# Asking for stored gate rows by pairs, and raising the priority of two steps, in a gated hybrid decoder step

## The chip, the cores and the metric

The kernel runs on one core of one Trainium2 chip. A core has a matrix engine (TensorE, PE here), a vector engine (VectorE, DVE), an engine for activations (ScalarE, ACT), GpSimd (POOL), and SyncE (SP), which here asks for nearly all DMA transfers. Each engine takes its own instructions in the order of the program and waits on semaphores for the others. The metric is the device time of one execution in microseconds (us); lower is better.

## The reference

One layer of a decoder step, on 1024 prompt tokens and on 64 sample tokens (8 requests of 8), with a model width of 1024. The sample tokens carry states; both groups use the same weights.

```
mod = silu(c) @ w_ada + b_ada                       # shifts, scales, gates
h = rmsnorm(x, g_norm1) * (1 + sc1) + sh1
rx, ry, sx, ga, gb = split(h @ w_in + b_in)
ra = rglru_branch(rx, ry, ...);  sb = s5_branch(sx, ...)
branch_a = ra @ w_rg_proj
glu_a, glu_b = split(sb @ w_glu)
branch_b = glu_a * sigmoid(glu_b)
merged = sigmoid(ga) * branch_a + sigmoid(gb) * branch_b
x = x + gt1 * (merged @ w_out)
h = rmsnorm(x, g_norm2) * (1 + sc2) + sh2
ua, ub = split(causal_dwconv(h @ w_up))
x = x + gt2 * ((gelu(ua) * ub) @ w_down);  y = rmsnorm(x, g_final)
```

The kernel computes the sigmoids as (tanh(v / 2) + 1) / 2. The change lies where `merged` is made and where the operands of `h @ w_up` are prepared.

## The kernel before

Everything is held transposed: eight row blocks m = 0 to 7 of 128 channels by tokens. The tokens go in two halves; half 0 is 512 prompt tokens and the 64 sample tokens (tiles of 128x576, two matmuls of 288 columns, L224), half 1 the other 512 prompt tokens (128x512, L226). Every fp32 operand is split into a hi and a lo part, and each product is three matmuls: hi by hi, lo by hi, hi by lo. For weights ACT makes the hi part (L176, `whi`) and DVE the lo part (L177, `wlo`) right after each load. For activations it is an ACT copy and a DVE subtraction too.

`strip` does two output blocks: it goes through the rows of X two at a time, and each chunk of weights serves two rows and two output blocks, 12 matmuls in half 1. After each chunk it calls `tick`, which lets background generators emit a few instructions. So background work and the main loop mix on the engines. The final order on each engine is set by a scheduler with priorities: an instruction has its place in program order, and `tc.high_priority(offset=k)` treats it as if it had been written k places earlier. Operands and buffers still bind.

The stretch that the change touches first is the GLU loop, one round for each pair b = 0 to 3 of row blocks. It multiplies by w_glu for columns 4 + b (gate side), and ACT puts the tanh into `q` (L1076). It multiplies for columns b (value side), and DVE makes (q + 1) * acc (L1081). Then for each of the two rows m it loads the stored gate row (`tgb`, written to DRAM earlier), makes (tgb + 1) * q (L1085), then 0.5 * q + bA (L1086), and splits the result into `mg` hi (ACT, L1088) and `mg` lo (DVE, L1089). `bA` is the other branch, made earlier. After the loop w_out multiplies `mg` (mg0 to mg7, in this order, two to a chunk) and adds the residual `xr`.

Loads into this loop and into the background generators share one tag of two buffers: `load_x` and `load_n` (L1095 to L1105) both take tag "ld". A third load thus waits until the first one's reader is done. In half 0's GLU a generator loads the second half's x (`xB`, later `xB2`) through these buffers, squares it (ACT, L347) and adds the squares into `accB` (DVE, L348), which PE sums over partitions (L357, `prs`). In half 1's GLU another generator (`h2a`) loads x after the first residual (`x2A`) through them and makes the operands `B11` and `B21` of the up-projection (L1157 ACT, L1158 DVE).

The up-projection multiplies 2 by 2 blocks in the manner of Strassen, with sums of activations as operands: `B11`, `B21`, `B22`, `T1` to `T4`, four row blocks each, made in `h2b` by a DVE subtraction (T3 at L1229, T4 at L1233) and the split (L1157, L1158). `up_lead` runs the first blocks while these are made, for two quads of output blocks; its last products are those with T2 (`p6`), with T3 (`p7`, L1251) and, for the first quad, with T4 (`p4`, L1248). DVE evacuates the results as `up` (L1405, L1408); a quad's `p4` writes where its `p7` has been evacuated. T4's forms live where the `h2B` tiles were, so T4 of a row can be made only after T3 of that row, and its second operand is loaded from DRAM (`hA`).

Of the kernel before, what the change touches and what calls it, by code (L numbers as in the profile page):

```python
# [8 lines left out]
F32 = mybir.dt.float32  # L9
F32R = mybir.dt.float32r  # L10
I32 = mybir.dt.int32
AF = mybir.ActivationFunctionType
OP = mybir.AluOpType
# [38 lines left out]
def _body(ctx, nc, tc, a):  # L52
    V, S, G, T_ = nc.vector, nc.scalar, nc.gpsimd, nc.tensor
# [157 lines left out]
    def strip(half, w, cb, X, nkb, kb0=0, tok=slice(0, 512)):  # L211

        T = [mm("mm0"), mm("mm1")] if half == 0 else [mm("mm")]
        for i, (hi, lo) in enumerate(weights(w, cb, range(kb0 // 2, (kb0 + nkb) // 2))):
            for m in range(2):
                c = slice(m * 128, (m + 1) * 128)
                for k in range(2):
                    x = X[2 * i + k]
                    first, last = i + k == 0, 2 * i + k == nkb - 1
                    for n, (y, r) in enumerate(((hi, 0), (hi, 1), (lo, 0))):  # L220
                        f = dict(start=first and n == 0, stop=last and n == 2)
                        if half == 0:
                            for h in range(2):
                                T_.matmul(T[m][:, h, :288], y[:, k, c], x[:, r, h * 288:(h + 1) * 288], **f)  # L224
                        else:
                            T_.matmul(T[0][:, m, tok], y[:, k, c], x[:, r, tok], **f)  # L226
            tick()
        return [Acc(half, T[m if half == 0 else 0], m) for m in range(2)]
# [799 lines left out]
    def part1(half, L, X, during_glu, ahead=None):  # L1028

        smp = half == 0  # L1030
        n = WID[half]
        sb = [None] * 4
        sxP = sx_strip(half, X, ahead)
        if smp:
            precompute_small()
        ra = [None] * 8
        H = []

        s5g = s5_blocks(half, sxP, sb)
        if not smp:  # L1040
            cold.append(s5g)
            other.append(adaB)
        for s in range(2):
            gate_strip(half, 0, s, X)
        for s in range(2):
            if s == 1 and smp:
                cold.append(s5g)
            g = rx_strip(half, s, X, H)
            gate_strip(half, 1, s, X)
            ry_strip(half, s, X, g, H, ra, L["RA"])  # L1050
        bA = []
        for b in range(4):
            if smp and b == 2:
                gt1 = ada_gen((4, 5), lambda: psum("ms", [128, 512], "sada"), adahl)
                other.append(gt1)
            acc = strip(half, a["w_rgp"], b, ra, 8)
            P2 = slot(L["BA"][b], f"bA{b}", F32)
            for j in range(2):
                m = 2 * b + j
                t = P2[:, j]  # L1060
                x = load_x(tgd[half][0][m * 128:(m + 1) * 128], "tga")
                with tc.high_priority(offset=400):
                    V.scalar_tensor_tensor(W(half, t), W(half, x), 1.0, acc[j].w, op0=OP.add, op1=OP.mult)
                bA.append(t)
        drain(s5g)
        if not smp:
            lead_weights()
        during_glu()
        merged = [None] * 8
        for b in range(4):  # L1070
            acc = strip(half, a["w_glu"], 4 + b, sb, 4)
            q = []
            for j in range(2):
                t = tmp("rx", [128, 664], f"q{j}", bufs=4)
                with tc.high_priority(offset=400):
                    S.activation(W(half, t), acc[j].w, AF.Tanh, scale=0.5)  # L1076
                q.append(t)
            acc = strip(half, a["w_glu"], b, sb, 4)
            for j in range(2):
                with tc.high_priority(offset=400):  # L1080
                    V.scalar_tensor_tensor(W(half, q[j]), W(half, q[j]), 1.0, acc[j].w, op0=OP.add, op1=OP.mult)  # L1081
            for j in range(2):
                m = 2 * b + j
                x, t = load_x(tgd[half][1][m * 128:(m + 1) * 128], "tgb"), q[j][:, :n]
                V.scalar_tensor_tensor(t, x, 1.0, t, op0=OP.add, op1=OP.mult)  # L1085
                V.scalar_tensor_tensor(t, t, 0.5, bA[m][:, :n], op0=OP.mult, op1=OP.add)  # L1086
                merged[m] = slot(L["MG"][m], f"mg{m}")
                S.activation(merged[m][:, 0, :n], t, AF.Copy, scale=0.5)  # L1088
                V.scalar_tensor_tensor(merged[m][:, 1, :n], t, 0.5, merged[m][:, 0, :n].bitcast(F32),  # L1089
                                       op0=OP.mult, op1=OP.subtract)  # L1090
        if smp:
            drain(gt1)
        return merged
# [6 lines left out]
    def load_x(src, name):  # L1100
        n = src.shape[1]
        t = (one("ld2", [128, 576], name, bufs=4) if two else tmp("ld", [128, 576], name, bufs=2))[:, :n]
        nc.sync.dma_start(t, src)
        return t
# [42 lines left out]
    def form(n, j):  # L1147
        if n in FORMS:
            x = slot(FORMS[n][j], f"{n}_{j}")
            x = x[:, :, :512] if n == "B22" else x  # L1150
        else:
            x = one(f"{n}_{j}", [128, 2, 512], f"{n}_{j}", F32R)
        F[n, j] = x
        return x

    def split_form(x, f):
        S.activation(x[:, 0], f, AF.Copy)  # L1157
        V.tensor_sub(x[:, 1], f, x[:, 0].bitcast(F32))  # L1158
# [48 lines left out]
    def h2b(ST):  # L1207

        A = []

        def load(tag, k, bufs):
            t = tmp(tag, [128, 632], "hA", bufs=bufs)[:, :576]
            nc.sync.dma_start(t, h2d[k])
            return t

        for j in range(4):
            norm_raw(ST[j][:, 1], ST[j][:, 1], rB2, 2 * j + 1)
            split_form(form("B22", j), ST[j][:, 1])
        for j in range(4):
            A.append(load("gl", 2 * j, 4))  # L1220
        for j in range(4):
            norm_raw(ST[j][:, 0], ST[j][:, 0], rB2, 2 * j)
            V.tensor_sub(A[j][:, 32:544], ST[j][:, 0], A[j][:, 32:544])
            split_form(form("T1", j), A[j][:, 32:544])
        for j in range(4):
            V.tensor_sub(A[j][:, 32:544], ST[j][:, 1], A[j][:, 32:544])
            split_form(form("T2", j), A[j])
        for j in range(4):
            V.tensor_sub(ST[j][:, 0], ST[j][:, 1], ST[j][:, 0])  # L1229
            split_form(form("T3", j), ST[j][:, 0])  # L1230
        for j in range(4):
            c = load("xc", 2 * j + 1, 3)
            V.tensor_sub(A[j], c, A[j])  # L1233
            split_form(form("T4", j), A[j])

    def prod(acc, kind, wt, n, start=False, stop=False):
        hi, lo = [x.rearrange("p (j c) -> p j c", c=128) for x in wt]
# [581 lines left out]
```

## Time and profile before

| | |
|---|---|
| median of 3 runs | 1747.87 us (1746.34 to 1749.92) |
| the profiled execution | 1748.04 us, its span in the trace 1746.3 us |
| PE busy | 1698.4 us, 97% |
| DVE busy | 1238.5 us, 71% |
| ACT busy | 913.3 us, 52% |
| DMA | 250.87 MB, 144 GB/s on average |

An engine's busy time is the sum of its instructions' durations. PE at 97% means that nearly all of the span is matmuls in a row, and that the other engines matter only where PE waits for them. A wait shows twice: in the list of waits, summed by the line that waited and what released it, and in the timeline, in brackets behind the instruction that came after it. Times in the timeline are counted from the start of the span. Line numbers in rows of the trace are those of the kernel before.

### The profile page before, as it was taken

Reading aid. Unit: us, or ns where it says so; the run is one execution under the profiler, and the core shown is the slowest. Engines: PE = TensorE matmul, PEld = TensorE weight load, DVE = VectorE, ACT = ScalarE, POOL = GpSimd, SP = SyncE. Lnnn points to the kernel's source line nnn. Section 1 sums busy time; section 2 is a strip of 40 time slices with the busy share of each in tenths; the row PEclk is TensorE's granted clock in tenths of the full one; section 3 lists DMA queues with packets and bytes.
Section 4 is the critical chain, followed back from the end, with each engine's and each line's share of the span. In section 5 each row is a group of like instructions: output and inputs, shape, how many; then the busy total and the mean of one; then the engine's idle time right before and its main releaser. Section 6 shows DMA issues by size and latency. Waiting matters only on the chain.

```text
span 1746.3 us, 29385 instructions
## 1 busy us (share of the span) xinstructions
PE 1698.4 (97%) x10542; PEld 1528.9 (88%) x10542; DVE 1238.5 (71%) x2629; ACT 913.3 (52%) x1608; POOL 230.6 (13%) x488
## 2 busy tenths in 40 slices
PE   7999999999999999999998999999999989999997
PEld 3899999998998777878786999999999979999887
DVE  8888688967855798665859877777777775336426
ACT  3556758535535588654536554555555545224224
POOL 0012110100100010020011422223322230000000
PEclk9999999999999999999999999999999999999999
DMA  8275334366546664455662222222222248445634
GB/s 305 70 237 178 97 109 145 105 196 209 178 145 195 210 190 147 122 157 162 217 224 94 77 81 81 80 75 75 75 75 74 76 136 287 133 134 172 195 95 136
DMA packets 151826, 250.87 MB, mean 144 GB/s; under 512 B 34048, under 2 KB 43264, under 8 KB 151680
## 3 DMA queue, kind: packets, MB, share of 16 engines
q1 hardware_dynamic: 151680, 248.99, 46.1%
q8 instruction: 83, 1.36, 0.3%
q14 instruction: 63, 0.52, 0.1%
HBM read 205.20 MB, written 43.73 MB: 143 GB/s over the span
## 4 chain that ended last, share of the span: by engine, by line
PE 69%; DVE 6%; DMA 3%; ACT 2%; issue 1%; POOLq 0%; SPq 0%; POOL 0%; DVEq 0%; ACTq 0%
PE mm L226 14%; PE mm L224 14%; PE b L1248 13%; PE e L1244 7%; PE mm L1541 7%; PE a L1248 4%; PE b L1251 3%; DMA al<-act 1%; DVE wlo L177 1%; PE pv L787 1%; PE pg L961 1%; DMA tgb<-tg 1%; PE sada L274 1%; PE sada L273 1%; DMA x2A<-x2d 1%
## 5 line engine op out<-in xcount | busy, mean ns | idle before, releaser
L176 ACT ACTIVATE whi<-raw 128x512 fp32r<-128x512 f32 x240 | 150.4, 627 | 218.8 <-PE mm L226 99.7
L177 DVE TENSOR_TENSOR wlo<-raw,whi 128x512 fp32r<-128x512 f32 x240 | 165.2, 689 | 123.6 <-ACT whi L176 103.7
L224 PE MATMUL mm<-h1A,whi 128*128 128x288 f32 x1024 | 182.9, 298 | 0.0
L226 PE MATMUL mm<-h1B,whi 128*128 128x512 f32 x512 | 159.8, 393 | 0.0
L177 DVE TENSOR_TENSOR wl<-raw,wh 128x512 fp32r<-128x512 f32 x105 | 72.0, 688 | 121.5 <-ACT wh L176 116.5
L224 PEld LDWEIGHTS mm<-h1A,whi 128*128 128x128 f32 x1024 | 151.1, 189 | 0.2
L224 PE MATMUL mm<-act,wh 128*128 128x288 f32 x768 | 135.8, 298 | 9.0 <-ACT act L1157 5.7
L176 ACT ACTIVATE wh<-raw 128x512 fp32r<-128x512 f32 x105 | 65.7, 628 | 143.1 <-PE mm L1541 81.7
L1248 PE MATMUL b<-T,wh 128*128 128x288 f32 x768 | 134.8, 296 | 4.8 <-DVE up L1408 1.8
L1541 PE MATMUL mm<-act,wh 128*128 128x512 f32 (+1 forms) x456 | 124.4, 361 | 0.0
L224 PEld LDWEIGHTS mm<-act,wh 128*128 128x128 f32 x768 | 114.2, 190 | 10.4 <-ACT act L1157 6.2
L1248 PEld LDWEIGHTS b<-T,wh 128*128 128x128 f32 x768 | 114.6, 188 | 8.4 <-DVE T L1158 2.1
L226 PEld LDWEIGHTS mm<-h1B,whi 128*128 128x128 f32 x512 | 95.6, 188 | 23.0
L245 ACT ACTIVATE wh<-wA 128x512 fp32r<-128x512 f32 x94 | 59.3, 630 | 105.5 <-PE b L1248 42.4
L224 PE MATMUL mm<-h1A,wlo 128*128 128x288 f32 x512 | 110.5, 296 | 2.5 <-DVE wlo L177 2.5
L246 DVE TENSOR_TENSOR wl<-wA,wh 128x512 fp32r<-128x512 f32 x94 | 65.3, 695 | 56.6 <-ACT wh L245 56.1
L226 PE MATMUL mm<-h1B,wlo 128*128 128x512 f32 x256 | 100.6, 393 | 0.7 <-DVE wlo L177 0.7
L1541 PEld LDWEIGHTS mm<-act,wh 128*128 128x128 f32 x456 | 80.7, 188 | 14.5 <-issue 0.5
L1386 DVE SCALAR_TENSOR_TENSOR gl<-up,vec,gl 128x624 f32<-128x624 f32 (+1 forms) x96 | 76.3, 806 | 14.2 <-ACT gl L1384 12.6
L1386 DVE SCALAR_TENSOR_TENSOR uc<-up,vec,uc 128x624 f32<-128x624 f32 (+1 forms) x96 | 75.8, 804 | 14.5 <-ACT uc L1384 11.4
L224 PEld LDWEIGHTS mm<-h1A,wlo 128*128 128x128 f32 x512 | 82.3, 188 | 2.7 <-DVE wlo L177 2.7
L224 PE MATMUL mm<-act,wl 128*128 128x288 f32 x384 | 83.2, 298 | 0.1
(452 smaller groups left out, 4351.1 us busy)
## 6 DMA issues: line engine op xcount, KB each, us to landing
raw<-w_in SPq DMA_DIRECT2D x128, 256.0 KB, 2.8
raw<-w_down SPq DMA_DIRECT2D x105, 256.0 KB, 2.7
wA<-w_up SPq DMA_DIRECT2D x94, 256.0 KB, 2.7
raw<-w_ada SPq DMA_DIRECT2D x56, 256.0 KB, 3.1
act<-uc SPq DMA_DIRECT2D x48, 256.0 KB, 2.1
araw<-w_ada SPq DMA_DIRECT2D x20, 512.0 KB, 7.2
s5a<-s5d SPq DMA_DIRECT2D x16, 512.0 KB, 4.0
raw<-w_rgp SPq DMA_DIRECT2D x32, 256.0 KB, 2.8
```

The lines of the kernel that those rows point to most:

```text
L176: S.activation(hi, raw, AF.Copy)
L177: V.tensor_sub(lo, raw, hi.bitcast(F32))
L224: T_.matmul(T[m][:, h, :288], y[:, k, c], x[:, r, h * 288:(h + 1) * 288], **f)
L226: T_.matmul(T[0][:, m, tok], y[:, k, c], x[:, r, tok], **f)
L245: S.activation(hi, src, AF.Copy)
L246: V.tensor_sub(lo, src, hi.bitcast(F32))
L273: T_.matmul(sa[:18], csr[:, kb], hi, start=kb == 0, stop=False)
L1244: T_.matmul(acc, w, x, **f)
L1248: T_.matmul(acc[:, h, :288], w, x[:, h * 288:(h + 1) * 288], **f)
L1251: T_.matmul(acc[:, h, o:o + 256], w, x[:, h * 256:(h + 1) * 256], **f)
L1386: V.scalar_tensor_tensor(dst, t[:, k:k + n], fw[:, k, m:m + 1], dst, op0=OP.mult, op1=OP.add)
L1541: T_.matmul(T[:, m, tok], y[:, k, c], act[kb][:, r, tok], start=kb + n == 0, stop=kb == 23 and n == 2, skip_group_check=True)
```

## The change

Three edits. Both gate rows of a pair are loaded before the second product of the pair, where each was loaded just ahead of its use. The four merge operations of the last pair (b = 3) get priority 600; the other pairs keep theirs. In `h2b`, the load, the subtraction and the split of T4 get priority 600.

```diff
--- before.py
+++ after.py
@@ -1075,19 +1075,21 @@
                 with tc.high_priority(offset=400):
                     S.activation(W(half, t), acc[j].w, AF.Tanh, scale=0.5)
                 q.append(t)
+            tgb = [load_x(tgd[half][1][m * 128:(m + 1) * 128], "tgb") for m in (2 * b, 2 * b + 1)]
             acc = strip(half, a["w_glu"], b, sb, 4)
             for j in range(2):
                 with tc.high_priority(offset=400):
                     V.scalar_tensor_tensor(W(half, q[j]), W(half, q[j]), 1.0, acc[j].w, op0=OP.add, op1=OP.mult)
             for j in range(2):
                 m = 2 * b + j
-                x, t = load_x(tgd[half][1][m * 128:(m + 1) * 128], "tgb"), q[j][:, :n]
-                V.scalar_tensor_tensor(t, x, 1.0, t, op0=OP.add, op1=OP.mult)
-                V.scalar_tensor_tensor(t, t, 0.5, bA[m][:, :n], op0=OP.mult, op1=OP.add)
+                x, t = tgb[j], q[j][:, :n]
                 merged[m] = slot(L["MG"][m], f"mg{m}")
-                S.activation(merged[m][:, 0, :n], t, AF.Copy, scale=0.5)
-                V.scalar_tensor_tensor(merged[m][:, 1, :n], t, 0.5, merged[m][:, 0, :n].bitcast(F32),
-                                       op0=OP.mult, op1=OP.subtract)
+                with tc.high_priority(offset=600 if b == 3 else 0):
+                    V.scalar_tensor_tensor(t, x, 1.0, t, op0=OP.add, op1=OP.mult)
+                    V.scalar_tensor_tensor(t, t, 0.5, bA[m][:, :n], op0=OP.mult, op1=OP.add)
+                    S.activation(merged[m][:, 0, :n], t, AF.Copy, scale=0.5)
+                    V.scalar_tensor_tensor(merged[m][:, 1, :n], t, 0.5, merged[m][:, 0, :n].bitcast(F32),
+                                           op0=OP.mult, op1=OP.subtract)
         if smp:
             drain(gt1)
         return merged
@@ -1229,9 +1231,10 @@
             V.tensor_sub(ST[j][:, 0], ST[j][:, 1], ST[j][:, 0])
             split_form(form("T3", j), ST[j][:, 0])
         for j in range(4):
-            c = load("xc", 2 * j + 1, 3)
-            V.tensor_sub(A[j], c, A[j])
-            split_form(form("T4", j), A[j])
+            with tc.high_priority(offset=600):
+                c = load("xc", 2 * j + 1, 3)
+                V.tensor_sub(A[j], c, A[j])
+                split_form(form("T4", j), A[j])
 
     def prod(acc, kind, wt, n, start=False, stop=False):
         hi, lo = [x.rearrange("p (j c) -> p j c", c=128) for x in wt]
```

No instruction is added or removed on any engine; they change places in three regions: half 0's GLU and w_out, half 1's GLU and w_out, and `up_lead`. Lines behind the edit are shifted by two to three: L1085, L1086, L1089 of before are L1088, L1089, L1091 of after; L1097 is L1099, L1103 is L1105, L1229 is L1231, L1158 is L1160, L1251 is L1254, L1405 and L1408 are L1408 and L1411.

In half 0, in the middle of the GLU, SP's queue has this before (`raw` are weight loads, `xB` the last loads of the second half's x, the two `tgb` rows those of pair 1):

```order
L1097 DMA xB_5545<-x 128x512
L184 DMA raw_5642<-w_ada 128x512
L197 DMA raw_5650<-w_glu 128x512
L1097 DMA xB_5588<-x 128x512
L1097 DMA xB_5637<-x 128x512
L184 DMA raw_5685<-w_ada 128x512
L197 DMA raw_5711<-w_glu 128x512
L1097 DMA xB_5680<-x 128x512
L184 DMA raw_5741<-w_ada 128x512
L1103 DMA tgb_5695<-tg01_123 128x576
L1103 DMA tgb_5702<-tg01_123 128x576
```

and now, from the same stretch on:

```order
L1099 DMA xB_5588<-x 128x512
L1105 DMA tgb_5605<-tg01_123 128x576
L197 DMA raw_5711<-w_glu 128x512
L184 DMA raw_5741<-w_ada 128x512
L1105 DMA tgb_5607<-tg01_123 128x576
L197 DMA raw_5751<-w_glu 128x512
L197 DMA raw_5804<-w_glu 128x512
L197 DMA raw_5843<-w_glu 128x512
L1099 DMA xB_5641<-x 128x512
L197 DMA raw_5896<-w_glu 128x512
L197 DMA raw_5935<-w_glu 128x512
L1099 DMA xB_5684<-x 128x512
```

The last xB moved from in front of the pair's two gate rows to behind them, and the one before it with it.

In half 1, at the end of the GLU, DVE's queue has this before (q0_9984 and q1_9986 are the rows m = 4 and 5, q0_10078 and q1_10080 the rows m = 6 and 7; mg4 had its last operation seven rows further up):

```order
L1085 SCALAR_TENSOR_TENSOR q1_9986<-tgb_10034,q1_9986 128x512
L1085 SCALAR_TENSOR_TENSOR q0_10078<-tgb_10121,q0_10078 128x512
L1086 SCALAR_TENSOR_TENSOR q1_9986<-q1_9986,bA2_9558 128x512
L177 TENSOR_TENSOR wlo_10194<-raw_10191,whi_10193 128x512
L1086 SCALAR_TENSOR_TENSOR q0_10078<-q0_10078,bA3_9638 128x512
L1089 SCALAR_TENSOR_TENSOR mg5_10038<-q1_9986,mg5_10038 128x512
L1085 SCALAR_TENSOR_TENSOR q1_10080<-tgb_10128,q1_10080 128x512
L1089 SCALAR_TENSOR_TENSOR mg6_10125<-q0_10078,mg6_10125 128x512
L1086 SCALAR_TENSOR_TENSOR q1_10080<-q1_10080,bA3_9638 128x512
L177 TENSOR_TENSOR wlo_10227<-raw_10224,whi_10226 128x512
L1089 SCALAR_TENSOR_TENSOR mg7_10132<-q1_10080,mg7_10132 128x512
```

and now:

```order
L1088 SCALAR_TENSOR_TENSOR q0_10078<-tgb_10082,q0_10078 128x512
L177 TENSOR_TENSOR wlo_10176<-raw_10173,whi_10175 128x512
L1089 SCALAR_TENSOR_TENSOR q0_10078<-q0_10078,bA3_9638 128x512
L1088 SCALAR_TENSOR_TENSOR q1_9986<-tgb_9990,q1_9986 128x512
L177 TENSOR_TENSOR wlo_10194<-raw_10191,whi_10193 128x512
L1091 SCALAR_TENSOR_TENSOR mg6_10125<-q0_10078,mg6_10125 128x512
L1088 SCALAR_TENSOR_TENSOR q1_10080<-tgb_10084,q1_10080 128x512
L1089 SCALAR_TENSOR_TENSOR q0_9984<-q0_9984,bA2_9558 128x512
L1089 SCALAR_TENSOR_TENSOR q1_10080<-q1_10080,bA3_9638 128x512
L1089 SCALAR_TENSOR_TENSOR q1_9986<-q1_9986,bA2_9558 128x512
L1091 SCALAR_TENSOR_TENSOR mg4_10031<-q0_9984,mg4_10031 128x512
L1091 SCALAR_TENSOR_TENSOR mg7_10130<-q1_10080,mg7_10130 128x512
```

The use of the last gate row (q1_10080<-tgb_10084, m = 7) now stands ahead of the second operation of m = 4 and of m = 5, and mg4 and mg5 are completed behind mg6. mg5's last operation is the row after this piece. On SP, three loads of x2A instead of one now stand between the gate rows of pair 1 and those of pair 2; the two gate rows of pair 3 come right behind those of pair 2, as before.

In the lead of the up-projection, DVE's queue has this before (T3 and T4 are the forms, h2B and hA their operands, `up` the evacuations):

```order
L1158 TENSOR_TENSOR T3_1_10748<-h2B1_10544,T3_1_10748 128x512
L1158 TENSOR_TENSOR T3_2_10752<-h2B2_10545,T3_2_10752 128x512
L246 TENSOR_TENSOR wl_10966<-wA21_9651,wh_10965 128x512
L1158 TENSOR_TENSOR T3_3_10756<-h2B3_10546,T3_3_10756 128x512
L246 TENSOR_TENSOR wl_10997<-wA21_10801,wh_10996 128x512
L1408 TENSOR_TENSOR up_10892<-e_10648,u2_10890 128x512
L1269 TENSOR_TENSOR S1_11082<-wA21_11076,wA22_11078 128x512
L1233 TENSOR_TENSOR hA_10695<-hA_10759,hA_10695 128x576
L1271 TENSOR_TENSOR S2_11084<-S1_11082,wA11_11074 128x512
L246 TENSOR_TENSOR wl_11028<-wA22_9653,wh_11027 128x512
L1408 TENSOR_TENSOR up_10941<-e_10648,u2_10939 128x512
```

and now, around the same second "up<-e,u" (up_10941):

```order
L1411 TENSOR_TENSOR up_10941<-e_10648,u2_10939 128x512
L1278 TENSOR_TENSOR S4_11087<-wA12_11080,S2_11084 128x512
L1160 TENSOR_TENSOR T3_1_10748<-h2B1_10544,T3_1_10748 128x512
L1231 TENSOR_TENSOR h2B2_10545<-h2B2_10545 128x512
L1231 TENSOR_TENSOR h2B3_10546<-h2B3_10546 128x512
L1160 TENSOR_TENSOR T4_1_10768<-hA_10697,T4_1_10768 128x576
L1160 TENSOR_TENSOR T3_2_10752<-h2B2_10545,T3_2_10752 128x512
L1160 TENSOR_TENSOR T3_3_10756<-h2B3_10546,T3_3_10756 128x512
L1389 SCALAR_TENSOR_TENSOR gl_10899<-up_10584,vec_78,gl_10899 128x624
L1160 TENSOR_TENSOR T4_2_10774<-hA_10699,T4_2_10774 128x576
L1408 TENSOR_TENSOR up_10993<-b_10505,p3_10799 128x512
L1160 TENSOR_TENSOR T4_3_10780<-hA_10701,T4_3_10780 128x576
```

Three of the four forms of T3 moved behind that evacuation, and T4's forms are mixed in among them; the four subtractions for T4 moved further up (not shown). The instructions ahead of the evacuation `up_11024<-b_10586,p3_10844` (the second quad's p7) are the same ones in both, in another order, and on DVE the two queues are nearly alike from there on. On PE, the p7 products of the two quads are mixed with each other.

## Rows read from the trace of the kernel before

**Rows 1.** Page, section 1: busy us of each engine, share, instructions.

```profile
PE 1698.4 (97%) x10542; PEld 1528.9 (88%) x10542; DVE 1238.5 (71%) x2629; ACT 913.3 (52%) x1608; POOL 230.6 (13%) x488
```

**Rows 2.** Waits of PE, 400 to 510: total us, times, longest us.

```profile
PE mm L224 <- ACT q L1076: 0.6, 1, 0.6
PE sada L274 <- DVE adahl L177: 0.5, 2, 0.3
```

**Rows 3.** Waits of PE, 810 to 980, same columns.

```profile
PE b L1248 <- DVE T L1158: 1.4, 3, 0.7
PE b L1248 <- DVE up L1405: 1.2, 1, 1.2
PE mm L226 <- ACT mg L1088: 1.2, 1, 1.2
...
PE mm L226 <- DVE mg L1089: 1.0, 2, 0.7
...
PE b L1248 <- ACT T L1157: 0.4, 1, 0.4
PE mm L226 <- DVE wlo L177: 0.2, 1, 0.2
```

**Rows 4.** Timeline, 419 to 436: start, us, engine, line, operation, count [idle before].

```profile
420.46 0.33 SPq L1097 DMA_DIRECT2D xB<-x  x1
...
423.85 1.49 DVE L348 TENSOR_TENSOR accB<-accB,sq 128x512 f32<-128x512 f32 x2
...
431.58 0.75 DVE L1085 SCALAR_TENSOR_TENSOR q<-tgb,q 128x576 f32<-128x576 f32 x1
...
432.36 0.33 SPq L1097 DMA_DIRECT2D xB<-x  x1
...
434.48 1.02 PE L357 MATMUL prs<-accB,ones 128*128 128x512 f32 x2
```

**Rows 5.** Tiles tgb, then xB: DMA from issue to landing.

```profile
DMA to landing us min/median/max: 2.7/3.6/4.6
...
DMA to landing us min/median/max: 2.5/3.0/5.0
```

**Rows 6.** Timeline, 853 to 868 (half 1, start of w_out).

```profile
854.25 0.62 PE L226 MATMUL mm<-mg,whi 128*128 128x512 f32 x2
...
854.93 0.62 PE L226 MATMUL mm<-mg,whi 128*128 128x512 f32 x2
...
855.44 1.28 DVE L1081 SCALAR_TENSOR_TENSOR q<-q,mm 128x512 f32<-128x512 f32 x2
...
859.17 1.29 DVE L1085 SCALAR_TENSOR_TENSOR q<-tgb,q 128x512 f32<-128x512 f32 x2
...
859.89 0.33 SPq L1103 DMA_DIRECT2D tgb<-tg  x1
...
861.78 0.49 PE L226 MATMUL mm<-mg,whi 128*128 128x512 f32 x1 [1.16 <-ACT mg L1088]
...
864.25 0.69 DVE L1085 SCALAR_TENSOR_TENSOR q<-tgb,q 128x512 f32<-128x512 f32 x1 [1.38 <-DMA tgb<-tg]
...
864.86 0.69 DVE L1089 SCALAR_TENSOR_TENSOR mg<-q,mg 128x512 fp32r<-128x512 f32 x1
...
866.17 0.63 ACT L1088 ACTIVATE mg<-q 128x512 fp32r<-128x512 f32 x1 [0.65 <-DVE q L1086]
```

**Rows 7.** Busy us in 930 to 958 (PE, PEld, DVE, ACT, POOL), then timeline, 936 to 960.

```profile
930.00:958.00 28.00, 25.13 (x156) 22.19 (x156) 27.63 (x44) 17.90 (x29) 1.09 (x2) 1.00 0.20 58
...
941.52 0.69 DVE L1158 TENSOR_TENSOR T<-h2B,T 128x512 fp32r<-128x512 f32 x1
...
945.04 0.64 PE L1251 MATMUL b<-T,wh 128*128 128x256 f32 x4
...
946.32 0.68 DVE L1408 TENSOR_TENSOR up<-e,u 128x512 f32<-128x512 f32 x1
...
957.42 0.68 DVE L1405 TENSOR_TENSOR up<-b,p 128x512 f32<-128x512 f32 x1
```

## The prediction

> **What bounds the kernel now.** I read the busy shares first: TensorE (PE) is busy 1698.4 of 1746.3 us [rows 1], so nothing matters that PE does not wait for. The profiled execution took 1748.04 us, 0.17 above the median of 1747.87; the sum below is made against 1748.04, of which 1746.3 is span. Next came PE's waits in the three stretches that the change reaches. In the first half's GLU and w_out the larger ones are 0.6 for ScalarE's tanh and 0.5 for the ada weights [rows 2]. In the second half's GLU, its w_out and the lead of the up-projection they are 1.2 and 1.0 us for merged rows, 0.2 for a weight half, 1.4 and 0.4 for the T forms and 1.2 for an evacuation [rows 3]. All else of PE's time there is work that the change does not touch: no instruction is added or taken away on any engine. So the change can give at most 2.2 + 1.8 = 4.0 us at the places at which it aims (w_out's merged rows and T4), and can cost whatever its new order makes PE wait. The third reading is the timelines around these waits, to see what each in-order queue does when instructions change places.
>
> **First half: two x rows are asked later.** During the first half's GLU a background generator loads the second half's x (xB), squares it and adds it into accB, which PE then multiplies by ones (L357). Before, the last xB was asked at 420.46, its add was one of the two at 423.85, and PE reached L357 at 434.48 without a wait: some 9 us of cover [rows 4]. Gate rows (tgb) and xB share two buffers. In the new SP order the last two xB come behind pair 1's two gate rows, so each must wait until one of those has been used. The use of the last one was the 0.75 us at 431.58, and the next load was asked the moment it ended, at 432.36 [rows 4]: I take that time for the last xB. xB lands 2.5 to 5.0 us after the ask, 3.0 in the median [rows 5]. Then come one pass of ScalarE, 0.63 [rows 6], and one add of VectorE, 0.75 (half of 1.49) [rows 4]: 432.36 + 3.0 + 0.63 + 0.75 = 436.74. PE wants accB at 434.48, so a wait of 2.3 us comes where none was; by the two ends of the landing 1.8 and 4.3. Against it, pair 1's tanh stood behind a square that waited for an xB; with the gate rows in front I count back the better part of that wait of 0.6, that is 0.5. **Term 1: +1.8, between +1.2 and +3.8.** The Trainium skill, "SBUF — State Buffer", section "The DMA setup-cost knee", says that each transfer pays a roughly fixed 2 us that mostly is completion latency. By 2 us the accB sum would end at 435.74 and the wait be 1.3; here no xB landed in under 2.5, so the trace decides.
>
> **Second half, GLU: weight halves behind late gate rows.** Every lo half of a weight (wlo) is made by VectorE in its queue, and so is every use of a gate row. Before, one x2A load stood between pair 1's and pair 2's gate rows; now there are three, all through the same two buffers, so pair 2's rows are asked late and VectorE stands at them with a wlo behind. Before, this cost PE 0.2 [rows 3]. The most that a VectorE instruction waited for a gate row there was 1.38 [rows 6]; if that lay wholly ahead of a wlo that PE wants, PE would pay it. The queue usually has a ready instruction in between, so I stay near the lower row. **Term 2: +0.5, between 0 and +1.4.**
>
> **Second half, w_out: the priority meets the last gate row.** This is the main term. Before, mg4 was complete soon after PE began w_out; the last gate row (m = 7) was asked at 859.89, when the use of m = 5 gave its buffer back (the first of the two passes at 859.17), and it was used at 864.25, after VectorE had waited 1.38 for it. The second op of m = 5 stood in front of that use, so PE waited just 1.16 at 861.78, for mg5 hi [rows 6], and 1.0 for two lo halves, the longer one 0.7 [rows 3]: 2.2 in all. In the new VectorE order, the use of m = 7 stands ahead of the second ops of both m = 4 and m = 5. VectorE takes its queue in order, so neither of these rows can be finished before the last gate row has landed; the priority puts the rows that PE wants last in front of those it wants next. Step by step:
> - The ask of m = 7 still needs m = 5's buffer. The use of m = 5 now stands behind that of m = 6, whose own ask needs m = 4's buffer, so it comes no earlier than before; I take 859.89 and the landing as measured, use at 864.25.
> - VectorE passes that wait for nothing start 0.61 apart (864.25 and 864.86) [rows 6]: m = 4's second op starts at 864.85 and ends at 865.54; ScalarE's pass of 0.63 makes mg4 hi by about 866.2.
> - PE began w_out at 854.25 [rows 6] and does one chunk of weights (two rows, 12 matmuls) in 2.73 us (groups of 0.68 by the starts 854.25 and 854.93 [rows 6], times four), so it wants mg4 at 854.25 + 5.46 = 859.7. It waits 6.5.
> - mg4 lo comes behind, about as mg5 lo did, 0.7, and the mg5 pair costs about the other 0.3: 7.5 in all, where 2.2 stood.
>
> So net +5.3. At best, m = 5's use follows the two passes at 855.44 with just m = 6's use between: 855.44 + 1.28 + 0.69 = 857.4 [rows 6]. The last row then lands 3.6 later [rows 5], at 861.0, and all moves up by 3.25: net +2.1. At worst it takes 4.6 instead of 4.36 [rows 5] and its ask is one pair of passes later (1.29, the two at 859.17): about +6.8. **Term 3: +5.3, between +2.1 and +6.8.** The Trainium skill, "Perfetto Trace Analysis", section "Optimization Strategy", says that gaps which repeat on the saturated engine can mean that too few buffers are there for the next tile. The row at 859.89 agrees: it is the buffer, not the place of the ask in the program, that sets when the last gate row comes, and the change adds no buffer.
>
> **Lead of the up-projection: a trade.** PE waited 1.8 us for T4 (1.4 for its lo halves, 0.4 for a hi half) and 1.2 for an evacuation, L1405 [rows 3], that VectorE did at 957.42 [rows 7]. With the priority T4 is early, and the T4 waits go. But in 930 to 958 VectorE is busy 27.63 of 28 us [rows 7], and the new order holds exactly the same instructions ahead of that same evacuation, in another order: T3's second to fourth forms now stand behind the second "up<-e,u" (946.32 before), while before all T3 forms had been made by 942.2 (941.52 + 0.69), and PE began on T3 at 945.04 [rows 7]. PE will wait for T3 instead. As the engine without slack reaches the evacuation at the same time, PE comes out of the region at the same time, about 958.1 (957.42 + 0.68). **Term 4: 0.** Where the T4 waits go and T3 costs nothing it is -1.8; where T3's forms come in pairs with gaps and the evacuation slips, I bound it by the four T3 passes of 0.69, +2.7.
>
> **Sum.** 1.8 + 0.5 + 5.3 + 0 = +7.6 us; 1748.04 + 7.6 = 1755.6. PE has little other waiting in which such delays could vanish [rows 2, 3].
>
> **The rivals.**
> - *It works as it is meant (faster).* One mechanism: the gate rows, asked before the second product, have landed when VectorE reaches them, so that the priority only moves ready work. Then w_out's 2.2 and T4's 1.8 vanish: 1748.04 - 4.0 = 1744.0. It decides at the last gate row: to have mg4 ready when PE wants it at 859.7, two passes of VectorE and ScalarE earlier (864.25 to 866.2 above, 2.0), it must land by 857.7, so be asked by 854.1 (3.6 landing), 5.8 us earlier than now. Against it: its buffer is m = 5's, and that was free only at 859.89. For it: the earlier pairs' rows are asked earlier, and in the lead the T4 part could come alone. Chance 6%.
> - *Nearly nothing.* The last gate row is asked at 857.4 (+2.1), xB lands in 2.5 (+1.2), T4's waits are gained (-1.8): 1748.04 + 1.5 = 1749.5. It needs three kind turns; 9%.
> - *The forecast,* with term 3 between its ends and the lead near zero: 1752.0 to 1759.5, likeliest 1755.6; 70%.
> - *Worse: T3 becomes a wait of its own.* T4's early subtractions push T3's forms past PE's need and the evacuation behind them slips by 2.7: 1755.6 + 2.7 = 1758.3, and with xB at 5.0 (+2.0) 1760.3; 15%.
>
> **How the numbers follow.** The range takes in the forecast and the worse case, and at the low end half of the "nearly nothing" case: 1750.5 to 1760.5, about 8 in 10 with what the unknown landings leave out. A measurement of this kernel tells about 0.2%, 3.5 us, from no change: below 1744.4 counts as faster, above 1751.4 as slower. Faster takes most of the first rival, 0.04; within 0.2% takes its rest, the "nearly nothing" case and a little of the forecast's low end, 0.13; slower takes the rest, 0.83.
>
> **What would show it.** In the profile after: a PE wait of 2 to 4 us at L357 for accB; in w_out a PE wait of 6 to 7 us for mg hi from ScalarE near 860 to 867, with VectorE standing at a gate row's use for its DMA just ahead; waits for T at L1248 gone or small, and L1254 (the products with T3) waiting instead, with the evacuation's wait still about 1.2. I am wrong if the last gate row is asked before 857, if accB shows no wait, or if VectorE has gaps in the lead, so that it could have done T3 earlier.

## The result, and where the time went

The changed kernel takes 1758.69 us (median of 4 runs, 1756.99 to 1761.94) against 1747.11 for the kernel before, measured with it (4 runs). The ratio is 1.0063, with a 95% interval of 1.0051 to 1.0076: 8.9 to 13.3 us slower. The forecast was 1755.6, in a range of 1750.5 to 1760.5.

The page after, in the lines that answer to [rows 1] (the span was 1746.3 before):

```profile
span 1756.7 us, 29390 instructions
...
PE 1703.9 (97%) x10542; PEld 1536.4 (87%) x10542; DVE 1237.0 (70%) x2629; ACT 914.7 (52%) x1608; POOL 236.4 (13%) x488
```

The span grew by 10.4 us. PE's busy time grew by 5.5 us, from 1698.4, with the same matmuls. So half of the loss is not waiting at all: the same instructions took longer. Where, is read best from a table by stage. The stages begin and end with the same matmuls in both kernels: half 0's GLU, half 0's w_out, half 1's GLU, half 1's w_out, the lead of the up-projection. The columns are the stretch, its length, the busy time (and count) of PE, PEld, DVE, ACT and POOL, the granted clock, the DMA share and GB/s. Before:

```profile
396.70:455.10 58.40, 57.34 (x412) 53.76 (x411) 45.05 (x68) 33.07 (x56) 1.24 (x2) 1.00 0.63 190
455.10:507.00 51.90, 51.65 (x386) 51.19 (x385) 33.17 (x67) 22.56 (x36) 3.13 (x1) 1.00 0.60 187
810.00:854.25 44.25, 44.06 (x195) 36.16 (x194) 35.41 (x63) 28.44 (x47) 0.00 (x0) 1.00 0.72 227
854.25:904.20 49.95, 47.74 (x208) 37.43 (x206) 29.07 (x45) 16.88 (x29) 1.29 (x1) 1.00 0.59 182
904.20:960.00 55.80, 50.75 (x291) 39.93 (x291) 51.55 (x77) 36.99 (x57) 10.04 (x16) 1.00 0.41 139
```

After:

```profile
397.30:460.00 62.70, 60.26 (x412) 56.12 (x411) 45.08 (x68) 34.24 (x58) 1.98 (x2) 0.95 0.61 181
460.00:513.40 53.40, 51.89 (x386) 51.23 (x385) 32.96 (x67) 21.81 (x35) 0.65 (x1) 1.00 0.59 177
816.10:860.69 44.59, 44.45 (x195) 36.03 (x194) 34.26 (x61) 28.91 (x46) 0.00 (x0) 1.00 0.66 215
860.69:914.70 54.01, 49.35 (x207) 39.42 (x205) 30.19 (x46) 17.64 (x29) 1.30 (x1) 0.94 0.55 179
914.70:970.50 55.80, 51.00 (x290) 40.12 (x290) 51.45 (x77) 36.83 (x57) 15.55 (x16) 1.00 0.42 136
```

| stage | longer by | PE idle more | PE busy more | clock after |
|---|---|---|---|---|
| half 0, GLU | 4.30 | 1.38 | 2.92 | 0.95 |
| half 0, w_out | 1.50 | 1.26 | 0.24 | 1.00 |
| half 1, GLU | 0.34 | -0.05 | 0.39 | 1.00 |
| half 1, w_out | 4.06 | 2.45 | 1.61 | 0.94 |
| lead | 0.00 | -0.25 | 0.25 | 1.00 |
| sum | 10.20 | 4.79 | 5.41 | |

Idle is length less busy. The two stages in which the clock was below 1.00 hold 8.4 of the 10.2 us.

**Half 0.** PE's waits that answer to [rows 2]:

```profile
PE prs L357 <- DVE accB L348: 2.2, 1, 2.2
PE mm L224 <- DVE rs L1111: 0.7, 1, 0.7
PE mm L224 <- ACT whi L176: 0.5, 1, 0.5
```

The wait for accB is there, where before there was none. In the timeline the last xB is asked when a gate row has been used (L1088 ended at 430.7), and everything behind it follows in turn:

```profile
430.70 0.39 SPq L1099 DMA_DIRECT2D xB<-x  x1
...
434.79 0.63 ACT L347 ACTIVATE sq<-xB 128x512 f32<-128x512 f32 x1 [0.54 <-DMA xB<-x]
...
435.45 0.69 DVE L348 TENSOR_TENSOR accB<-accB,sq 128x512 f32<-128x512 f32 x1
...
436.20 2.06 PE L357 MATMUL prs<-accB,ones 128*128 128x512 f32 x2 [2.22 <-DVE accB L348]
```

It landed some 4 us after its ask, PE waited 2.22, and then the two matmuls of L357 took 2.06 us where they had taken 1.02 [rows 4]. That is the clock, at its lower level (0.5 is 1.2 GHz, 1.0 is 2.4 GHz):

```profile
436.00:442.00 6.00, 5.80 (x19) 4.26 (x20) 3.72 (x5) 3.44 (x5) 0.00 (x0) 0.52 0.43 131
```

It came back within 442 to 444 (0.73 in those 2 us). Later, in half 0's w_out, PE waited 0.71 for an evacuation that had waited for its residual row (xr), which passes through the same two buffers:

```profile
475.52 0.88 DVE L1124 SCALAR_TENSOR_TENSOR xo<-mm,modT,xr 128x224 f32<-128x224 f32 x2 [0.78 <-DMA xr<-x]
...
476.68 0.78 PE L224 MATMUL mm<-mg,whi 128*128 128x288 f32 x4 [0.71 <-DVE rs L1111]
```

**Half 1's w_out.** The waits that answer to [rows 3], for merged rows and in the lead:

```profile
PE mm L226 <- ACT mg L1090: 4.3, 1, 4.3
PE b L1254 <- DVE T L1160: 1.5, 2, 1.1
PE b L1251 <- DVE up L1408: 1.1, 1, 1.1
```

The timeline shows the inversion that answers to [rows 6]: the last gate row asked (865.70), the use of m = 5's (866.79), the use of the last one (868.60), and only then the second ops of m = 4, 7 and 5 (869.20), their hi halves, and PE, which had wanted mg4 at 866.3:

```profile
865.70 0.32 SPq L1105 DMA_DIRECT2D tgb<-tg  x1
...
866.79 0.68 DVE L1088 SCALAR_TENSOR_TENSOR q<-tgb,q 128x512 f32<-128x512 f32 x1
...
868.60 0.69 DVE L1088 SCALAR_TENSOR_TENSOR q<-tgb,q 128x512 f32<-128x512 f32 x1
869.20 1.89 DVE L1089 SCALAR_TENSOR_TENSOR q<-q,bA 128x512 f32<-128x512 f32 x3
...
869.92 1.84 ACT L1090 ACTIVATE mg<-q 128x512 fp32r<-128x512 f32 x3 [2.38 <-DVE q L1089]
...
870.60 0.80 PE L226 MATMUL mm<-mg,whi 128*128 128x512 f32 x1 [4.31 <-ACT mg L1090]
```

From the use of m = 4's gate row to these second ops, with the columns of the stages:

```profile
861.00:869.20 8.20, 5.29 (x24) 4.05 (x22) 8.03 (x14) 2.95 (x5) 0.00 (x0) 1.00 0.74 230
```

VectorE was busy 8.03 of the 8.20 us. The forecast has it standing at the last gate row, and it did not: the use at 868.60 follows the instruction before it without a gap, and the only wait for a gate row in the stretch is one of 0.17 us at 864.98. What held mg4 back was the work that stood ahead of it in VectorE's queue, the last pair's among it.

Behind that wait of 4.31 the clock was again at its lower level, until shortly after 876:

```profile
870.00:876.00 6.00, 5.04 (x11) 3.59 (x12) 2.90 (x5) 1.76 (x3) 0.00 (x0) 0.50 0.25 81
```

**The lead** took 55.80 us in both. As forecast, the T4 waits are gone, PE waits 1.5 for T3 instead, and the evacuation still holds it for 1.1. VectorE was busy 27.57 of the 28 us from 941 to 969. The evacuation on which PE waits (957.42 before) came 10.45 us later, and the lead itself began 10.5 us later. The rows that answer to [rows 7]:

```profile
967.87 0.68 DVE L1408 TENSOR_TENSOR up<-b,p 128x512 f32<-128x512 f32 x1
...
968.70 0.77 PE L1251 MATMUL b<-T,wh 128*128 128x288 f32 x4 [1.14 <-DVE up L1408]
```

### The profile page after: what moved, and what is told of

Read it like the earlier page. It is cut to its first block, busy times and chain, and to the rows that moved or that the text cites. A ratio compares the mean times of both kernels' runs of the same rounds, so it can differ in the third digit from the quotient of the medians.

```text
span 1756.7 us, 29390 instructions
## 1 busy us (share of the span) xinstructions
PE 1703.9 (97%) x10542; PEld 1536.4 (87%) x10542; DVE 1237.0 (70%) x2629; ACT 914.7 (52%) x1608; POOL 236.4 (13%) x488
## 3 DMA queue, kind: packets, MB, share of 16 engines
q8 instruction: 83, 1.36, 0.3%
## 4 chain that ended last, share of the span: by engine, by line
PE 70%; DVE 7%; DMA 2%; issue 1%; ACT 1%; POOLq 0%; SPq 0%; POOL 0%; DVEq 0%; ACTq 0%
PE mm L224 15%; PE mm L226 15%; PE b L1251 13%; PE e L1247 7%; PE mm L1544 7%; PE a L1251 4%; PE b L1254 3%; DVE wlo L177 1%; PE pg L961 1%; PE pv L787 1%; PE sada L274 1%; PE prs L357 1%; DMA xB<-x 1%; PE sada L273 0%; DVE adahl L177 0%
## 5 line engine op out<-in xcount | busy, mean ns | idle before, releaser
L1251 PE MATMUL b<-T,wh 128*128 128x288 f32 x768 | 134.0, 296 | 2.9 <-DVE up L1411 1.8
L1251 PEld LDWEIGHTS b<-T,wh 128*128 128x128 f32 x768 | 114.5, 188 | 5.7 <-issue 1.9
```

The source lines that it names most:

```text
L1251: T_.matmul(acc[:, h, :288], w, x[:, h * 288:(h + 1) * 288], **f)
```

## The experiments

Times are medians; "before" is the kernel before, run beside the experiments on the same chip: 1748.98 us (30 runs) for e1 to e4, 1748.53 (35) for e5 to e8, 1749.03 (27) for e9 to e12. The ratios are to that.

**One edit at a time.** e1 is the changed kernel without its two priorities:

```diff
-                with tc.high_priority(offset=600 if b == 3 else 0):
+                with tc.high_priority(offset=0):
...
-            with tc.high_priority(offset=600):
-                c = load("xc", 2 * j + 1, 3)
+            c = load("xc", 2 * j + 1, 3)
```

> Only the first edit: both gate rows of a pair asked before the second product; no raised priorities. Theory (two shared buffers and queues in order; a long PE wait also costs granted clock): half 0 is as in the changed kernel, PE waits about 2.2 us at L357 for accB, the granted clock falls behind it, +4 us there and +1 to +1.5 in half 0's w_out. In half 1 the second ops of m = 4 and 5 stand ahead of the last gate row again, so PE's waits for mg stay under 2.5 us in all and the clock is not lost there. About +6 us, between +4 and +8. Rival (the late asks alone make w_out stall, the priority is innocent): the wait of over 4 us for mg hi remains and the time is +9 to +11.

1751.64 us, 1.0019 (1.0009 to 1.0029), some 3.3 us slower, a little less than expected. The wait for accB is as in the changed kernel, but the clock was not lost behind it:

```profile
436.58 1.12 PE L357 MATMUL prs<-accB,ones 128*128 128x512 f32 x2 [2.09 <-DVE accB L348]
```

```profile
438.00:440.00 2.00, 2.00 (x16) 2.00 (x16) 0.55 (x4) 1.84 (x2) 0.00 (x0) 1.00 0.55 154
```

In half 1, PE waits 1.4 us for mg, and a weight half comes late:

```profile
PE mm L226 <- DVE wlo L177: 1.8, 1, 1.8
...
PE mm L226 <- ACT mg L1090: 1.0, 1, 1.0
...
PE mm L226 <- DVE mg L1091: 0.4, 1, 0.4
```

So the long wait in w_out does not come with the early asks alone; the rival falls. The late weight half costs 1.8 us, above term 2's bound of 1.4, but not by term 2's mechanism: ahead of it VectorE had stood 2.96 us (until 836.84) at an instruction of h2A that waited for a store of h2A (h2d), not at a gate row. In the changed kernel the same stop took 1.07 us and no weight half came late.

e2 is the second edit alone, against the kernel before:

```diff
+                with tc.high_priority(offset=600 if b == 3 else 0):
+                    V.scalar_tensor_tensor(t, x, 1.0, t, op0=OP.add, op1=OP.mult)
...
```

> Only the second edit: priority 600 for the merge of the last pair, each gate row asked just ahead of its use as before. Theory: nothing changes in half 0 (no wait at L357). In half 1 mg5 is finished behind the use of the last gate row, so PE waits for mg hi some 2 to 4 us where 1.2 stood; net +1 to +2 by the wait, up to +5 if the granted clock falls behind it. Rival (the priority is innocent): PE's waits for mg stay at 2.2 us or fall, time within 1 us of before.

1754.75 us, 1.0029 (1.0019 to 1.0038), 5.1 us slower. Half 0 has no wait at L357. Half 1's w_out took 54.60 us against 49.95, with the clock at 0.94, and holds one wait for mg hi of the same length as in the changed kernel:

```profile
866.47 1.52 PE L226 MATMUL mm<-mg,whi 128*128 128x512 f32 x2 [4.33 <-ACT mg L1089]
```

```profile
854.80:909.40 54.60, 49.62 (x207) 39.32 (x205) 29.64 (x45) 17.05 (x28) 1.29 (x1) 0.94 0.55 169
```

The priority of the last pair is enough for the long wait and for the fall of the clock behind it. Here it is m = 5 whose first op is queued behind the last gate row's use, and VectorE stood at no gate row: it was busy 9.23 of the 9.30 us from 856.4 to 865.7.

e3 is the third edit alone:

```diff
-            c = load("xc", 2 * j + 1, 3)
+            with tc.high_priority(offset=600):
+                c = load("xc", 2 * j + 1, 3)
...
```

> Only the third edit: priority 600 for the making of T4. Theory (VectorE without slack in the lead): the 1.8 us of waits for T4 at L1248 go, about 1.5 us of waits for T3 come at the p7 products, and the evacuation's wait of about 1.2 stays: time within 1 us of before. Rival (the T4 waits are a true gain that the other edits hide): -1.5 to -1.8 us.

1748.36 us, 0.9995 (0.9985 to 1.0004). In the profile the waits for T4 are gone, 1.5 us for T3 and 1.1 for the evacuation stand in their place, and the lead ends as before. The theory holds.

**The order, or the buffers?** e4 is the changed kernel, with the gate rows in the ring of seven buffers of tag "rg":

```diff
+    def load_g(src, name):
+        t = rg(name)[:, :src.shape[1]]
+        nc.sync.dma_start(t, src)
+        return t
...
-            tgb = [load_x(tgd[half][1][m * 128:(m + 1) * 128], "tgb") for m in (2 * b, 2 * b + 1)]
+            tgb = [load_g(tgd[half][1][m * 128:(m + 1) * 128], "tgb") for m in (2 * b, 2 * b + 1)]
```

Of the loads of the merge, that is tgb alone; xr stays where it was.

> All three edits, and the gate rows tgb and the loads of load_x in the GLU's merge take another ring of buffers (the seven of tag rg) in place of the two of tag ld. Theory: the last xB no longer waits for a gate row's use, so the wait at L357 and the clock fall behind it go; the scheduler finishes mg4 and mg5 ahead of the last pair, PE waits under 1.5 us for mg, no clock fall in w_out: between -2.5 and +1.5 us against before. Rival (the priorities as such cost, whatever the buffers): +4 us or more, with a wait of over 3 us for mg.

1750.03 us, 1.0003 (0.9994 to 1.0012). Both waits are gone, for accB and for mg, and so is the loss of 11 us; with other buffers the scheduler also places the second ops of m = 4 and 5 ahead of the last pair. It gains nothing on the kernel before, since a weight half (1.9 us in half 1's w_out) and ada's weights (2.1 in half 0) are late instead.

e5 leaves the two buffers and the early asks as they are and changes one number:

```diff
-                with tc.high_priority(offset=600 if b == 3 else 0):
+                with tc.high_priority(offset=600 if b >= 2 else 0):
```

> The changed kernel with priority 600 for the merges of the last two pairs (m = 4 to 7) in place of the last one: the rows then are finished in the order in which w_out takes them, with the same two buffers and the same early asks. Theory (the inversion, not the priority or the buffers, makes w_out's long wait): PE's waits for mg in half 1's w_out fall from 4.7 to under 2.5 us, no clock is lost there, w_out is at least 3 us shorter than in the changed kernel; half 0 keeps its wait of about 2.2 at L357. Against before +2 to +6 us. Rival (late asks by the two buffers set the wait): the wait for mg stays over 3.5 us and the time at +9 or more.

1749.66 us, 1.0005 (0.9996 to 1.0014): better than the lower end that was expected. With m = 4 to 7 in the order of need, w_out is 49.00 us, 5 us shorter than in the changed kernel, at full clock:

```profile
857.50:906.50 49.00, 47.80 (x208) 37.55 (x206) 29.88 (x46) 17.17 (x29) 1.29 (x1) 1.00 0.65 196
```

```profile
PE mm L226 <- DVE mg L1091: 0.7, 1, 0.7
PE mm L226 <- ACT mg L1090: 0.5, 2, 0.3
```

This separates order from buffers: the buffers are the same, the last gate row is asked 4.9 us behind PE's start on w_out (862.43) where it was 5.0 in the changed kernel, and the long wait is gone. Half 0 still waits for accB, 2.38 us, and again without a fall of the clock behind it in the profiled execution: half 0's GLU took 60.10 us there, 1.7 more than before, with PE's busy time the same within 0.1.

e6 raises the last two pairs in half 1 only, keeps the third edit, and asks for gate rows as before:

```diff
-                with tc.high_priority(offset=600 if b == 3 else 0):
+                with tc.high_priority(offset=600 if half == 1 and b >= 2 else 0):
```

> The second and third edit alone, the second one for half 1 only and for the last two pairs (m = 4 to 7); gate rows asked just ahead of their use as before. Theory: half 0 as before; in half 1's w_out mg4 to mg7 are made in the order of need, waits for mg fall from 2.2 to about 1; the lead is even. Against before -2 to +0.5 us. Rival (raised merges push weight halves back): waits for wlo or whi grow by as much as the waits for mg shrink, or more: 0 to +3 us.

1748.64 us, 1.0002 (0.9993 to 1.0011). PE no longer waits for mg at all, but for weight halves, as the rival said:

```profile
PE mm L226 <- DVE wlo L177: 3.6, 2, 3.1
```

The longer of the two, 3.08 us, ended at 859.39, and the clock did not fall behind it:

```profile
860.00:862.00 2.00, 2.00 (x10) 1.65 (x9) 2.00 (x4) 0.79 (x2) 0.00 (x0) 1.00 0.68 238
```

e7 has none of the edits, and only the gate rows in the ring of seven (the `load_g` of e4, in the kernel before):

> None of the three edits, but the gate rows tgb and the other loads of load_x in the merge come from the ring of seven buffers in place of the ring of two. Theory (the buffers set when gate rows come): VectorE no longer waits 1.4 us for the last gate row, PE's waits for mg in half 1 fall from 2.2 to under 1; no clock fall; -2.5 to +1 us against before. Rival (the ring of seven makes other work wait): squares and h2A forms are late, time +1 us or more.

1751.20 us, 1.0014 (1.0005 to 1.0023). Half 1's w_out is 3.7 us shorter, 46.20, without a wait; but half 0's w_out is 5.5 us longer, with a wait of 2.6 us for mg hi and the clock at 0.97:

```profile
456.60:514.00 57.40, 53.69 (x386) 52.75 (x385) 34.70 (x69) 22.64 (x36) 2.44 (x2) 0.97 0.53 165
862.90:909.10 46.20, 46.20 (x207) 37.84 (x205) 26.11 (x39) 16.08 (x27) 2.04 (x3) 1.00 0.55 170
```

The ring moves the wait from one half to the other. Its rival holds in sum, though what came late was another row of the merge, not squares or forms.

**What a wait costs.** e8, e9 and e10 are the kernel before, with 10, 12 and 15 passes of GpSimd over accB that delay it:

```diff
             yield
+        for _ in range(10):
+            G.tensor_scalar(acc, acc, 1.0, 0.0, op0=OP.mult, op1=OP.add)
         yield
```

e9 and e10 carry a second edit, which their expectations do not name: at the end of half 0's `sx_strip`, some 360 us ahead of L357, they call `tick` 12 and 15 times in place of 10 (e9 is shown). So their whole times are not the price of the wait alone, and that price is read below from the stage in which the wait lies.

```diff
-              for _ in range(10):
+              for _ in range(12):
                 tick()
```

> The kernel before with ten passes of GpSimd over accB, each times 1.0, ahead of the sum at L357: they only delay accB. By GpSimd's 1.3 us for an addition over 128x512 in the lead PE would wait some 4 us at L357. Theory (a long wait also costs granted clock): the time grows by the wait and about 3 us more, and the granted clock behind L357 is 0.5 for several us. Rival: the time grows by the wait alone, with the clock at 1.0 behind it.

This run was mis-sized: a pass took 0.98 us and not 1.3, so PE waited 0.15 us at L357. 1750.82 us, 1.0009 (0.9998 to 1.0020). It tells nothing of a long wait, but what the passes cost without one: half 0's GLU took 60.30 us, 1.9 more than before, with waits of 2.2 us for ada's weights where 0.5 stood, at full clock.

> The kernel before with twelve passes of GpSimd over accB, each times 1.0, ahead of the sum at L357 (a pass took 0.98 us with ten of them, and PE's wait was 0.2). PE should wait 1.5 to 2.5 us at L357, about as in the changed kernel. Theory (a wait of this length can cost granted clock, but need not): against before +1.5 to +2.5 us by the wait, up to +5.5 where the clock falls behind it too. Rival (the fall of the clock belongs to what the changed kernel does around it, not to the wait): +1.5 to +2.5 us, clock 1.0 behind L357 in the profile.

1752.85 us, 1.0026 (1.0017 to 1.0035), some 4.5 us. PE waited as long as in the changed kernel, and the clock fell behind it, for a shorter stretch:

```profile
436.45 1.13 PE L357 MATMUL prs<-accB,ones 128*128 128x512 f32 x2 [2.25 <-POOL accB L1622]
```

```profile
438.00:440.00 2.00, 2.00 (x10) 1.96 (x9) 1.82 (x3) 0.30 (x1) 0.00 (x0) 0.50 0.45 131
```

> The same with fifteen passes: PE should wait 4.5 to 5.5 us at L357. Theory (a long wait costs the wait and granted clock behind it): +7.5 to +9 us against before, with the clock at 0.5 for some 6 us behind L357. Rival: +5 us, the wait alone.

1757.51 us, 1.0052 (1.0038 to 1.0066), some 9 us for a wait of 5.05:

```profile
440.62 2.08 PE L357 MATMUL prs<-accB,ones 128*128 128x512 f32 x2 [5.05 <-POOL accB L1622]
```

```profile
442.00:444.00 2.00, 2.00 (x8) 1.34 (x8) 0.69 (x3) 0.69 (x1) 0.00 (x0) 0.50 0.00 0
```

Half 0's GLU in e9 and in e10, where the kernel before took 58.40 us with PE busy 57.34:

```profile
395.60:458.60 63.00, 59.21 (x411) 55.27 (x410) 48.27 (x68) 33.10 (x57) 12.45 (x14) 0.97 0.58 176
...
398.40:464.10 65.70, 59.94 (x411) 55.81 (x411) 48.46 (x67) 32.74 (x56) 14.80 (x17) 0.95 0.57 168
```

The stage became 4.6 and 7.3 us longer, and 1.9 and 2.6 us of that are the same matmuls taking longer, behind waits of 2.25 and 5.05; in e8, almost without the wait, PE's busy time there grew by 0.25. So a late operand alone is enough for a fall of the clock, and the rival, by which the fall belongs to something else in the changed kernel, falls. The Trainium skill, "TensorE: Matmul & The Clock Gate", section "HAM oscillation — how this bites in real kernels", says that waits between bursts of matmuls send the clock down, and that each return is paid for; e10 agrees, with 2.6 us of slower matmuls behind a wait of 5.05, but no fall came behind the 3.08 us of e6.

**Is VectorE what holds the lead?** e11 is e3 with T4's four subtractions on GpSimd:

```diff
-                V.tensor_sub(A[j], c, A[j])
+                G.tensor_sub(A[j], c, A[j])
```

> The third edit alone, with T4's four subtractions on GpSimd in place of VectorE. Theory (VectorE without slack sets the end of the lead): 3 us of VectorE work leave the lead, so the evacuation of the second quad comes earlier, and of PE's waits there (1.5 for T3 and 1.1 for the evacuation with the third edit alone) at least 1 us goes: -1 to -2.5 us against before. Rival (PE waits for T4's loads or for GpSimd instead, 1.3 to 1.7 us an addition): 0 to +2 us.

1749.95 us, 1.0009 (0.9999 to 1.0018). The evacuation's wait fell from 1.1 to 0.3 and T3's from 1.5 to 0.5, as the theory has it, but a new wait of 2.7 us came earlier in the lead, so that nothing is gained (1.0 of the 3.7 below stood in e3 too). PE waited for a copy by ScalarE. GpSimd's subtractions took about 2 us each, and ScalarE stood 3.15 us, until 936.00, for the second of them, with that copy behind it in its queue. So the rival holds, by way of ScalarE:

```profile
PE e L1245 <- ACT p L1308: 3.7, 2, 2.7
...
PE b L1252 <- ACT T L1157: 0.5, 1, 0.5
PE b L1249 <- DVE up L1406: 0.3, 1, 0.3
```

```profile
931.64 4.32 POOL L1234 TENSOR_TENSOR hA<-hA 128x576 f32<-128x576 f32 x2 [9.51 <-DVE T L1158]
```

e12 puts together what had looked best: half 0 as before, e5's order in half 1, e11's lead.

> The parts put together: half 0 as before; in half 1 the gate rows by pairs and priority 600 for the merges of m = 4 to 7; T4 with priority and its subtractions on GpSimd. Theory: no wait for accB, waits for mg under 2 us, lead shorter by 1 to 2.5: -1 to -3.5 us against before. Rival (weight halves wait behind late gate rows in half 1's GLU, as 1.8 us with the first edit alone): 0 +-1.5 us.

1750.37 us, 1.0006 (0.9997 to 1.0015). No wait for accB, 1.1 us for mg, and the lead's new waits as in e11. No variant beats the kernel before by what can be measured.

## Why the prediction came out as it did

- **The direction and the inversion held, but not what was to make the inversion cost.** The use of the last gate row ahead of what PE wants next (e2 alone shows it, e5 removes it) and the two x rows that wait for gate rows (e1) are the loss. But the forecast let the landing of the last gate row set the time, with VectorE standing at it; VectorE stood 0.17 us at gate rows and was busy for the rest of 8.20 us, and in e2, from 856.4 on, at none. So one of the signs named in the forecast did not come, and the order of the queue delayed mg4, not the load. The faster rival needed the last gate row to be asked by about 854, no later than PE's start on w_out; it was asked at 865.70, 5.0 us behind that start.
- **Term 1, half 0: the wait was right, its price was not.** Forecast a wait of 2.3, measured 2.22. Two steps behind it were off and cancelled: the last xB was asked at 430.70, not 432.36, but took some 4 us to land, not 3.0; and PE was there 0.5 us earlier than before. PE's idle time grew by 1.4, near the +1.8 of the sum. What the step left out is the clock: PE's busy time in that stage grew by 2.9. The term came to +4.3, above its upper end of 3.8. This is the step that failed; the sum took a wait to cost what it lasts.
- **A term was missing.** Half 0's w_out became 1.5 us longer. The 0.71 of it that is shown above follows from a residual row that came late; the other 0.5 and 0.3 are weight halves. Why that row was late is not shown: e5 has the 0.7 too, e1, with nearly the same wait for accB, does not.
- **Term 2: +0.5 forecast, +0.3 measured, and the nearness is luck.** PE waited for no weight half in that stage: its idle time fell by 0.05, and the 0.3 is busy time. VectorE did stand 1.36 us at a gate row there (847.90), with no late weight half behind it.
- **Term 3, w_out: too much waiting, no clock.** Forecast +5.3, all of it waiting (6.5 for mg4, 7.5 in all); measured +4.1, of which 2.45 is waiting (4.31 for mg4) and 1.6 is slower matmuls. The ask did not need m = 5's buffer: it came at 865.70, as soon as m = 6's use had ended and before m = 5's (866.79). And the row was used 2.9 us after its ask and without a wait for it, where I had taken the 4.36 of the trace of before, 1.38 of them a wait for the row. From the use to PE's first matmul it took 2.0 us, as worked out.
- **Term 4, the lead: 0 forecast, 0.00 measured,** by the reasons given; e3 alone says the same.
- **Nothing that hides it.** The delays went through to the end, as forecast: 10.2 us in the five stages, 10.4 in the span.

The sum was 7.6, the span's growth 10.4. Of the waits the sum held too much by about 2.8 (7.6 against 4.8 of idle time), and it held none of the 5.4 us by which matmuls ran slower. The two errors were of unlike sign, and so the time came out within 3.1 us.

**What stays open.** Waits at L357 of 2.09 (e1) and 2.38 us (e5) were followed by full clock in their profiled executions, waits of 2.22 (changed kernel) and 2.25 (e9) by the lower one, for 6 and 3 us. So the length of the wait alone does not decide it there, nor elsewhere: full clock followed waits of 3.08 us in e6 and of 2.48 us in the kernel before (for a weight half, until 217.53), and the same wait for ScalarE's copy in the lead was followed by the lower clock in e11 (2.69 us) and by full clock in e12 (2.71). Over all runs the mean granted clock was 0.990 in the changed kernel (0.989 to 0.991 in four), 0.993 in e1 (0.991 to 0.995) and 0.994 in e5 (0.992 to 0.995), 0.993 in the kernel before. That suggests that e1's and e5's waits rarely cost clock, but such a mean takes in the whole execution and does not show it; the reason was not found.

## What to carry to other kernels

A raised priority on an in-order engine pushes back whatever stood ahead: before giving it, look at who is queued behind, and whether the matrix engine wants that first. Raise the whole run in the order of its need, as e5 does, or none. Look too at how much slack that engine has: here PE waited 4.31 us for it while it stood for 0.17. And where the matrix engine is nearly always busy, let the upper end of a sum hold more than the length of a long wait on it: behind four such waits here (2.22, 2.25, 4.31 and 5.05 us) matmuls took 1.6 to 2.9 us longer, behind others (2.09, 2.38 and 3.08) they did not. Look at the clock column of the stage before closing the sum.

## What the hardware showed that was not expected

The clock fell behind waits of 2.04 (the changed kernel, for a weight half, until 216.66), 2.22, 2.25, 2.69 (e11), 4.31, 4.33 (e2) and 5.05 us, for 3 to 7 us each time, and did not behind waits of 2.09 (e1), 2.38 (e5), 2.48 (before), 2.71 (e12) and 3.08 us (e6). The same matmul pair (L357) took 1.02 us before, 2.06 and 2.08 behind waits of 2.22 and 5.05, and 1.12 or 1.13 behind waits of 2.09, 2.25 and 2.38. In e9 and e10, with PE waiting 2.25 and 5.05 us for one operand, half 0's GLU became 4.6 and 7.3 us longer. GpSimd took 0.98 us for a multiply and add of one tile over 128x512 (e8), and about 2 us for a subtraction of two tiles over 128x576 in the lead (e11), where VectorE was busy 14.56 of 15 us; whether the second operand or the busy VectorE makes the difference, these runs do not tell.
